# Gates and values of a hybrid decoder block computed first, partly by seven products, and kept in DRAM

## The chip, the core and the metric

The kernel runs on one core of one Trainium2 chip. The core has a matrix engine (TensorE, PE in the profile; its weight loads are listed as PEld), a vector engine (VectorE, DVE), an engine for activation functions (ScalarE, ACT), a general one (GpSimd, POOL) and an engine that mostly issues DMAs (SyncE, SP). Each runs its own instructions in their order; semaphores tie them together. Operands of matmuls lie in SBUF, results in PSUM (eight banks of 128 x 512 floats). Weights stream in from DRAM. The metric is the time of one execution in microseconds on the device; the kernel before takes 1744.1 us, the median of three runs (1743.35 to 1745.33).

## What is computed

One layer for 256 tokens of width 2048, in float32, cut to what matters:

```python
a = rmsnorm(h, norm_mix_pre)
proj = a @ w_in                                   # 2048 x 17408
q_a, k_a, v_a, q_r, f_r, i_r, g_r, gate_a, gate_r = split_columns(proj)
qh, kh, vh = rotary(heads(q_a)), rotary(heads(k_a)), heads(v_a)   # 3 groups x 8 heads x 128
for g, (window, dilation) in enumerate(((128, 1), (512, 4), (2048, 16))):
    o_g, lse_g = dilated_window_attention(qh[g], kh[g], vh[g], window, dilation)
attn = sum over g of softmax(lse over g) * o_g
q = silu(q_r); f = lb + (1 - lb) * sigmoid(f_r)
r = hgrn2_chunked(q, log(f), 1 - f, i_r)          # S_t = diag(f_t) S_{t-1} + k_t v_t, o_t = S_t q_t
r = rmsnorm per head(r) * gain * silu(g_r)
y = sigmoid(gate_a) * (attn @ w_attn_branch) + sigmoid(gate_r) * (r @ w_hgrn_branch)
h = h + rmsnorm(y @ w_mix_out, norm_mix_post)
a = rmsnorm(h, norm_ffn_pre)
h = h + rmsnorm((silu(a @ w_gate) * (a @ w_up)) @ w_down, norm_ffn_post)   # width 5632
```

## The kernel before

**Products in three parts.** Every weight tile is split into a high part (ScalarE, a copy to the matmul type) and a low part (VectorE, the difference), the activations too, and a product is three matmuls: high x high, high x low, low x high. The weights arrive in 512 KB loads from SP into three buffers of 1 MB, are split two steps ahead (`AHEAD`), and are multiplied from three buffers `w`.

**Blocks.** A block is a stretch of columns that owns PSUM banks. Kind "N" (`add`) makes 512 columns with tokens on the partitions: eight steps of 12 matmuls of 128x512. Kind "W" (`add_wide`, two blocks of 256 columns each) makes columns on the partitions and tokens along the row, for f, q of the recurrence and for queries and keys: four steps of 16 matmuls, half of them 512 and half 256 wide; `both_halves` adds the two halves of a bank and hands the result to an evacuation. Blocks of 1024 columns (`add_wide_block`, class `Wide`) are used for up/gate and down. In three of the eight steps of an up/gate block (`GATE_UP`), the two halves of the tokens, the two row tiles and the two column groups form a 2 x 2 product that is made with seven products instead of eight (Strassen's way, Winograd's form): `split_wide` then splits sums of weights as well, `seven_sums` the sums of activations, and `gather` adds the four banks that hold shared products. Such a step has 21 matmuls instead of 24. The down blocks have more of them.

**The order of work.** `chunks` lists the steps of the first half in order, `steps` those of the `Wide` blocks. After each step's matmuls the loop advances the evacuations (`evacs`) and two `lanes` by one `yield` each. A lane holds generators in a row: `opening` (norm of x, tables), the two recurrences (`recurrence(half)`, four heads each), and `attention(half, h)`. Each generator puts a few small instructions on several engines and yields, so that its matmuls fall between the steps of the blocks. The order in the first half is: g (two N blocks), f and q of the recurrence (eight W), inputs i (two N), then for each half of the heads the values of three groups (three N) and queries and keys (twelve W), then the gates (eight N), the branch products, the mix product. The recurrences start when q is done, so the first runs beside i and the values of the first half, the second beside queries and keys of the first half; the attention of a half starts when its last keys are there, the second one beside the gates, whose sigmoids wait until the heads are done (`gate_sigmoids`).

**A level of the recurrence** (`level`, six per recurrence, then `same`, `level64`, `level128`): POOL subtracts (`L769`), ScalarE takes exponentials, VectorE and POOL multiply (`L775`, `L776`), eight small matmuls, VectorE copies under a mask (`L786`). A new level starts every second step.

**Even and odd tokens.** The attention works on even and odd tokens apart. The value blocks therefore read `xT` with a stride of two (`parity=True`), the last addition of the rotation (`evac_rope`, `L683`) writes its result sorted, and the end of a head sorts back. In the rest the token halves are the first and the last 128.

Of the kernel before, what the change touches and what calls it, by code (L numbers as in the profile page):

```python
# [19 lines left out]
P = 128  # L20
# [20 lines left out]
N_RAW, N_SPLIT, AHEAD, WARM, BRIDGE = 6, 3, 2, 8, 6  # L41


class Block:
# [7 lines left out]
    def __init__(self, kind, w, nk, col, xs, evac, parity=False, pre=None, mid=None, post=None):  # L52
        self.kind, self.w, self.nk, self.col = kind, w, nk, col
        self.xs, self.evac, self.parity = xs, evac, parity
        self.pre, self.mid, self.post = pre, mid, post
        self.per = 4 if kind == "W" else 2
        self.width = 1024 // self.per
        self.steps = nk // self.per
        self.banks = None


class Wide:
# [7 lines left out]
    def __init__(self, w, cols, order, xs, seven, evac, prep=None, pre=None, turn=1):  # L70
        self.w, self.cols, self.order, self.xs, self.seven = w, cols, order, xs, seven
        self.evac, self.prep, self.pre, self.turn = evac, prep, pre, turn
        self.last7 = max(i for i, (m, s) in enumerate(order) if s)
        self.bank, self.open, self.rest = {}, set(), None
# [3 lines left out]
def tile_hybrid_block(ctx: ExitStack, tc: tile.TileContext, t, out):  # L78
# [8 lines left out]
    auxp = ctx.enter_context(tc.tile_pool(name="auxp", bufs=4, space=PSUM))  # L87
    ctx.enter_context(tc.manual_schedule())
# [19 lines left out]
    def p3(s, dtype, n, bufs, tag=None):  # L108
        return act_pool[0].tile([P, n], dtype, tag=tag or s, bufs=bufs, name=nm(s))
# [40 lines left out]
    colg = cpool.tile([P, 48], F32, name="colg")  # L150
    r1c = cpool.tile([P, 2], F32, name="r1c")
    r1p = cpool.tile([P, 2], F32, name="r1p")
# [5 lines left out]
    ph1 = ExitStack()  # L158
    kp = ph1.enter_context(tc.tile_pool(name="kp", bufs=1, reuse_waits="tile"))
    fp = ph1.enter_context(tc.tile_pool(name="fp", bufs=1, reuse_waits="tile"))  # L160

    act_pool = []

    def fslot(s):
        return fp.tile([P, 1024], F32, tag="f", bufs=15, name=nm(s))

    def ptile(s):
        pool, n = (act_pool[0], 2) if act_pool else (fp, 5)
        return pool.tile([P, 512], F32, tag="p", bufs=n, name=nm(s))
# [9 lines left out]
    lb = kp.tile([P, 8], F32, name="lb")  # L179
    lb1 = kp.tile([P, 8], F32, name="lb1")  # L180


    blocks, chunks, pairs = [], [], []
    wides, steps = [], []

    def add(*args, **kw):
        b = Block(*args, **kw)
        blocks.append(b)
        for c in range(b.steps):
            chunks.append([b, c, None, None, None])  # L190
# [15 lines left out]
    def parts(j):  # L206

        return (slice(0, 512), slice(512, 1024)) if j == 0 else (slice(0, 1024),)

    def load(j):  # L210
        if j >= len(chunks):
            load_wide(j - len(chunks))
            return
        b, c = chunks[j][:2]
        if j % 2 == 0:
            pairs.append(stream.tile([P, 2048], F32, tag="raw", bufs=N_RAW // 2, name=nm("raw")))
        raw = pairs[j // 2][:, j % 2 * 1024 : j % 2 * 1024 + 1024]
        rows = b.per * P
        src = b.w[c * rows : (c + 1) * rows, b.col : b.col + b.width]
        src = src.rearrange("(k p) c -> p k c", p=P)  # L220
        dst = raw.rearrange("p (k c) -> p k c", k=b.per)
        n = len(parts(j))
        for i in range(n):
            ks = slice(i * b.per // n, (i + 1) * b.per // n)
            nc.sync.dma_start(dst[:, ks, :], src[:, ks, :])
        chunks[j][2] = raw
# [4 lines left out]
    def split(j, only=None):  # L231
        if j >= len(chunks):
            split_wide(j - len(chunks))
            return
        raw = chunks[j][2]
        if chunks[j][3] is None:
            w = wslot()
            chunks[j][3:] = [w[:, :1024], w[:, 1024:]]
        wh, wl = chunks[j][3:]
        for n, k in enumerate(parts(j)):  # L240
# [4 lines left out]
    def multiply(j, sides=(0, 1)):  # L245
        b, c = chunks[j][:2]
        wh, wl = (w.rearrange("p (k c) -> p k c", k=b.per) for w in chunks[j][3:])
        if b.banks is None:
            b.banks = [acc_bank() for _ in range(2)]
        for s in sides:  # L250
            if s == 1 and c == 0 and b.mid:
                b.mid()
            for kk in range(b.per):
# [20 lines left out]
    def add_wide_block(*args, **kw):  # L274
        b = Wide(*args, **kw)
        wides.append(b)
        for i in range(len(b.order)):
            steps.append([b, i, None, None])

    def load_wide(n):  # L280
        if n % 2 or n // 2 >= len(steps):
            return
        n //= 2
        b, i = steps[n][:2]
        m = b.order[i][0]
        raw = stream.tile([P, 2048], F32, tag="raw", bufs=N_RAW // 2, name=nm("raw"))
        for g, col in enumerate(b.cols):
            src = b.w[2 * m * P : (2 * m + 2) * P, col : col + 512]
            nc.sync.dma_start(
                raw[:, g * 1024 : (g + 1) * 1024].rearrange("p (k c) -> p k c", k=2),  # L290
                src.rearrange("(k p) c -> p k c", p=P),
            )
        steps[n][2] = raw

# [1144 lines left out]
```

## Time and profile before

The profiled execution took 1742.44 us, 1740.6 of them inside the span. Stretches of the span, from the windows of the trace:

| us from the start | work | TensorE busy | VectorE busy | ScalarE busy | POOL busy |
|---|---|---|---|---|---|
| 0 to 57 | start, g | 55.4 | 35.8 | 35.7 | 2.8 |
| 57 to 147 | f, q of the recurrence | 90.0 | 55.2 | 43.7 | 0 |
| 147 to 277 | i, first values; first recurrence | 129.7 | 81.9 | 66.0 | 32.9 |
| 277 to 434 | first queries, keys; second recurrence | 155.3 | 127.5 | 71.4 | 34.6 |
| 434 to 521 | second values; attention | 87.0 | 42.9 | 40.1 | 0 |
| 521 to 661 | second queries, keys | 140.0 | 102.4 | 61.3 | 0 |
| 661 to 850 | gates; attention | 189.0 | 93.9 | 87.7 | 0 |
| 850 to 1077 | branches, mix, start of the second half | 224.7 | 143.1 | 112.3 | 3.8 |
| 1077 to 1500 | up and gate, seven products | 423.0 | 368.2 | 228.9 | 0 |
| 1500 to 1741 | down | 231.5 | 214.0 | 139.2 | 0 |

In rows of groups the columns are line, engine, operation, output and inputs, shape, count, busy time and mean in ns, and the idle time before them with what ended it. In rows of the timeline they are start, duration and instruction. A row of the windows gives, after the stretch, its length and the busy time of PE, PEld, VectorE, ScalarE and POOL with their counts, then the granted clock of TensorE, the busy share of the DMA engines and GB/s. In the chain of waits the columns are start, duration and what ran. Float32 matmuls, unlike those of the matmul type, are listed twice.

### The profile page before, as it was taken

To read this page: it belongs to the slowest core of one execution; us is meant where nothing else is said; L and a number is where in the kernel's file an instruction comes from. 1 tells how busy PE (TensorE), PEld (TensorE's weight loads), DVE (VectorE), ACT (ScalarE), POOL (GpSimd) and SP (SyncE) were. 2 spreads that over 40 slices of the span, in tenths; PEclk is the share of its full clock that TensorE was granted. 3 is DMA by queue.
4 is the path that set the end of the run, shared out by engine and by line. 5 is a ranking of instruction groups with operands and counts; after the bars stand their busy time and mean duration, and the time that the engine had idled before them with its cause. 6 is when DMAs were issued, how large, how long until landed. Compare 5 with 4: busy or idle time off the path is not lost.

```text
span 1740.6 us, 21588 instructions
## 1 busy us (share of the span) xinstructions
PE 1725.5 (99%) x8424; PEld 1448.5 (83%) x8424; DVE 1264.6 (73%) x1372; ACT 886.2 (51%) x1050; POOL 74.1 (4%) x54
## 2 busy tenths in 40 slices
PE   9999999999999999999999999999999999999997
PEld 7888888888888888888888877888888888888886
DVE  5657747877546775544566577888888888898998
ACT  6545455344444444454444466555555555665663
POOL 0001413400000000000000000000000000000000
PEclk9999999999999999999999999999999999999999
DMA  7655445445454554445555745655555555666553
GB/s 268 202 194 194 145 149 165 146 157 183 169 167 155 188 193 169 170 169 193 191 180 187 266 166 176 214 198 200 206 194 194 194 194 199 220 209 218 194 198 116
DMA packets 201222, 325.91 MB, mean 187 GB/s; under 512 B 10096, under 2 KB 76832, under 8 KB 201120
## 3 DMA queue, kind: packets, MB, share of 16 engines
q1 hardware_dynamic: 198848, 319.41, 54.3%
q10 hardware_dynamic: 2272, 5.12, 0.8%
q8 instruction: 66, 1.08, 0.3%
q14 instruction: 36, 0.29, 0.1%
HBM read 322.40 MB, written 2.10 MB: 186 GB/s over the span
## 4 chain that ended last, share of the span: by engine, by line
PE 95%; DVE 2%; ACT 1%; DMA 1%; issue 1%; POOL 0%; SPq 0%; DVEq 0%; ACTq 0%
PE acc L115 71%; PE aux L115 22%; DVE w L243 1%; ACT w L242 0%; DVE w L676 0%; PE aux L723 0%; PE aux L452 0%; DMA gpost<-in_norm_mix_post 0%; DMA x<-in_x 0%; PE acc L1126 0%; DVE fz L1255 0%; PE aux L1126 0%; DVE x L775 0%; PE aux L439 0%; ACT junk L1209 0%
## 5 line engine op out<-in xcount | busy, mean ns | idle before, releaser
L243 DVE TENSOR_TENSOR w<-raw,w 128x1024 fp32r<-128x1024 f32 (+1 forms) x353 | 444.6, 1260 | 365.5 <-ACT w L242 363.4
L242 ACT ACTIVATE w<-raw 128x1024 fp32r<-128x1024 f32 (+1 forms) x353 | 373.0, 1057 | 481.6 <-PE acc L115 471.0
L115 PE MATMUL acc<-w,xT 128*128 128x512 f32 x1728 | 407.7, 394 | 0.0
L115 PEld LDWEIGHTS acc<-w,xT 128*128 128x128 f32 x1728 | 325.0, 190 | 65.5
L115 PE MATMUL acc<-xT,w 128*128 128x512 f32 (+1 forms) x2048 | 364.5, 339 | 0.0
L115 PEld LDWEIGHTS acc<-xT,w 128*128 128x128 f32 x2048 | 313.8, 189 | 46.2
L307 DVE TENSOR_TENSOR wl<-raw,w 128x2048 fp32r<-128x2048 f32 x82 | 187.5, 2287 | 34.0 <-ACT w L305 34.0
L305 ACT ACTIVATE w<-raw 128x2048 fp32r<-128x2048 f32 x82 | 156.6, 1910 | 81.7 <-PE aux L115 32.2
L115 PE MATMUL acc<-w,hT 128*128 128x512 f32 x622 | 182.5, 392 | 1.5 <-DVE w L243 1.2
L115 PEld LDWEIGHTS acc<-w,hT 128*128 128x128 f32 x622 | 115.8, 188 | 27.0 <-DVE w L243 2.4
L115 PE MATMUL aux<-w,hT 128*128 128x512 f32 x430 | 135.6, 389 | 0.0
L323 DVE TENSOR_TENSOR wl<-sum,w 128x2048 fp32r<-128x2048 f32 x42 | 96.2, 2290 | 33.8 <-ACT w L319 33.8
L316 ACT ACTIVATE w<-sum 128x1024 fp32r<-128x1024 f32 x42 | 44.7, 1063 | 111.0 <-DVE sum L311 106.7
L115 PEld LDWEIGHTS aux<-w,hT 128*128 128x128 f32 x430 | 80.7, 188 | 16.7
L115 PE MATMUL acc<-w,yT 128*128 128x512 f32 x384 | 88.0, 390 | 0.1
L115 PEld LDWEIGHTS acc<-w,yT 128*128 128x128 f32 x384 | 71.9, 188 | 15.3 <-DVE w L243 0.5
L115 PE MATMUL aux<-w,a 128*128 128x512 f32 x268 | 83.7, 389 | 0.0
L115 PE MATMUL acc<-w,a 128*128 128x512 f32 x268 | 83.6, 389 | 0.0
L115 PE MATMUL aux<-wl,hT 128*128 128x512 f32 x215 | 83.6, 389 | 0.0
L115 PE MATMUL acc<-wl,hT 128*128 128x512 f32 x215 | 83.6, 389 | 0.0
L325 DVE TENSOR_TENSOR dl<-raw,dh 128x1536 fp32r<-128x1536 f32 x42 | 73.6, 1751 | 0.0
L322 ACT ACTIVATE dh<-raw 128x1536 fp32r<-128x1536 f32 x42 | 61.9, 1474 | 0.0
(263 smaller groups left out, 2014.9 us busy)
## 6 DMA issues: line engine op xcount, KB each, us to landing
raw<-in_w_in SPq DMA_DIRECT2D x271, 512.0 KB, 4.5
raw<-in_w_ffn_gate_up SPq DMA_DIRECT2D x176, 512.0 KB, 4.4
raw<-in_w_ffn_down SPq DMA_DIRECT2D x88, 512.0 KB, 4.8
raw<-in_w_mix_out SPq DMA_DIRECT2D x32, 512.0 KB, 4.9
raw<-in_w_attn_branch SPq DMA_DIRECT2D x16, 512.0 KB, 4.7
raw<-in_w_hgrn_branch SPq DMA_DIRECT2D x16, 512.0 KB, 4.5
hx<-in_x ACTq DMA_DIRECT2D x4, 512.0 KB, 9.8
x<-in_x SPq DMA_DIRECT2D x3, 512.0 KB, 10.3
```

The source lines that it names most:

```text
L115: nc.tensor.matmul(ps, lhsT, rhs, start=start, stop=stop, skip_group_check=True)
L242: nc.scalar.activation(wh[:, k], raw[:, k], AF.Copy)
L243: nc.vector.tensor_sub(wl[:, k], raw[:, k], wh[:, k].bitcast(F32))
L305: nc.scalar.activation(hi, raw, AF.Copy)
L307: nc.vector.tensor_sub(lo, raw, hi.bitcast(F32))
L316: nc.scalar.activation(hi[:, :1024], s[:, :1024], AF.Copy)
L322: nc.scalar.activation(dhi, d, AF.Copy)
L323: nc.vector.tensor_sub(lo, s, hi.bitcast(F32))
L325: nc.vector.tensor_sub(dlo, d, dhi.bitcast(F32))
```

## The change

1. Right after g, eight blocks of 1024 columns come first: the four pieces of the two branch gates, the values of the three groups, the inputs i. The first is made of plain steps (`FIRST`), the other seven have the order of the up/gate blocks (`EIGHT`) with three steps of seven products. The sums of activations for three pairs of `xT` are made in a lane by `pair_sums`.
2. Their results, and g, are scaled or passed through the sigmoid (`evac_kept`, ScalarE) and stored to DRAM tiles by ScalarE's queue. They are loaded back by POOL's queue when they are needed (`back`, `values_back`, `gate_back`).
3. Partition p of a token tile now holds the tokens 2p and 2p + 1, so the two token halves are the even and the odd tokens, everywhere. `parity`, `r1p` and the sorting in the rotation and in the attention go; f and q of the recurrence are sorted into time order by their first multiplication, and the recurrence's result back by `put(..., timed=True)`.
4. Queries and keys are made for pairs of heads: per pair three groups of one W block of queries and one of keys, and the attention of a pair starts when its three groups are done. Heads wait in `work` and go to whichever lane is empty; the branch product of the attention asks for them (`heads`).
5. f and q come per half, and each recurrence starts when its own q is done. In a level, one `yield` more stands between the multiplications and the matmuls, and the rotation's two sine products are parted by a `yield`.
6. The branch of the recurrence comes ahead of that of the attention. One list `seq` of `Step`s replaces `chunks` and `steps`. The pools of the first half are opened for two stages, "early" and "middle" (`enter`).

The matrix products are otherwise the same. The core of the diff:

```diff
-H7 = (0, 1, 2)
-GATE_UP = [(3, 0), (4, 0), (0, 1), (5, 0), (1, 1), (6, 0), (2, 1), (7, 0)]
+X7 = H7 = (0, 1, 2)
+FIRST = [(m, 0) for m in range(8)]
+EIGHT = [(3, 0), (4, 0), (0, 1), (5, 0), (1, 1), (6, 0), (2, 1), (7, 0)]
...
                 if b.kind == "N":
                     ps = b.banks[s]
-                    if b.parity:
-                        sh, sl = (
-                            x.rearrange("p (j two) -> p two j", two=2)[:, s, :]
-                            for x in (xh, xl)
-                        )
-                    else:
-                        sh, sl = (x[:, s * P : (s + 1) * P] for x in (xh, xl))
+                    sh, sl = (x[:, s * P : (s + 1) * P] for x in (xh, xl))
...
-    xv = t["x"][0].rearrange("(b p) c -> p b c", p=P)
+    xv = t["x"][0].rearrange("(p b) c -> p b c", b=2)
+    ov = out[0].rearrange("(p b) c -> p b c", b=2)
...
+    def keep(key, width):
+        kept[key] = dram.tile([S, width], F32, name=nm("kept"))
+        return kept[key].rearrange("(p b) c -> p b c", b=2)
+
+    def back(dst, key, lo, hi, timed=False):
+        x = kept[key]
+        x = x.rearrange("(b p) c -> p b c", b=2) if timed else x.rearrange("(p b) c -> p b c", b=2)
+        nc.gpsimd.dma_start(dst, x[:, :, lo:hi])
+
+    def evac_kept(key, fn):
+        def go(b):
+            dst = keep(key, 1024)
+            for s, g in ((0, 0), (0, 1), (1, 0), (1, 1)):
+                src = b.bank[s, g]
+                if b.rest:
+                    e = b.rest[s, g]
+                    nc.vector.tensor_add(e, src, e)
+                    src = e
+                else:
+                    e = eslot()
+                nc.scalar.activation(e, src, fn, scale=r1c[:, s : s + 1])
+                nc.scalar.dma_start(dst[:, s, g * 512 : (g + 1) * 512], e)
+            yield
+        return go
+
+    def end_early():
+        flush(evacs)
+        enter("middle")
+        attnT.append(Split("attnT", 8))
+        recT.append(Split("recT", 8))
+        for half in range(2):
+            gN[half] = hslot("g")
+            back(gN[half], ("g", half), 0, 512, True)
+            iN[half] = hslot("v")
+            back(iN[half], "i", 512 * half, 512 * half + 512, True)
+
+    def values_back(half):
+        for g in range(3):
+            vN[half, g] = hslot("v") if half == 0 and g < 2 else nslot("v")
+            back(vN[half, g], ("v", g), 512 * half, 512 * half + 512)
...
             w = ptile("w").rearrange("p (h t) -> p h t", h=2)
-            for o, n in ((0, 64), (64, 0)):
+            for m, n in ((0, 64), (64, 0)):
                 nc.vector.tensor_mul(
-                    w[o : o + 64], src[n : n + 64],
+                    w[m : m + 64], src[n : n + 64],
                     sin[n : n + 64, None, :].to_broadcast([64, 2, S]),
                 )
+                if m == 0:
+                    yield
...
             nc.vector.tensor_mul(xv[:, :, left], xv[:, :, left], kv[:, :, left])
             nc.gpsimd.tensor_mul(xv[:, :, right], xv[:, :, right], qv[:, :, right])
             yield
+            yield
             ps = aux()
...
+    early = [(COL_GA, ("a", 0), AF.Sigmoid), (COL_GB, ("r", 0), AF.Sigmoid),
+             (COL_GA + 1024, ("a", 1), AF.Sigmoid), (COL_GB + 1024, ("r", 1), AF.Sigmoid)]
+    early += [(COL_V + 1024 * g, ("v", g), AF.Copy) for g in range(3)] + [(COL_IR, "i", AF.Copy)]
+    for n, (col, key, fn) in enumerate(early):
+        add_seven(w_in, (col, col + 512), EIGHT if n else FIRST, xT, lambda m: x7[m],
+                  evac_kept(key, fn), flip=n % 2 == 1, turn=1,
+                  pre=flush_lanes if n == 1 else None)
     for half in range(2):
         add_wide(w_in, KD, COL_FR + 512 * half, xT, evac_f(half))
-    for half in range(2):
-        add_wide(w_in, KD, COL_QR + 512 * half, xT,
-                 evac_qr(half, start_recurrence if half == 1 else None))
-    for half in range(2):
-        add("N", w_in, KD, COL_IR + 512 * half, xT, scaled(iN, half, r1c, hslot))
...
+        if half == 0:
+            blocks[-2].pre = end_early
+        add_wide(w_in, KD, COL_QR + 512 * half, xT, evac_qr(half, start_recurrence(half)))
+    for pair in range(4):
         for g in range(3):
...
+            for o, col, tab in ((0, COL_Q, 0), (2, COL_K, 2)):
+                then = start_attention(pair) if o and g == 2 else None
+                add("W", w_in, KD, col + 1024 * g + 256 * pair, xT,
+                    both_halves(evac_rope((pair, g), o, tab, then), 0))
+    blocks[-3].pre = lambda: (gate_back("r", 0), gate_back("r", 1))
     for j in range(4):
-        add("N", w_in, KD, COL_GA + 512 * j, xT, evac_gate(("a", j), hslot))
+        add("N", t["w_hgrn_branch"][0], 8, 512 * j, lambda k: recT[0](k), evac_rec_branch(j))
+    for j, (key, n) in enumerate((("r", 2), ("a", 0), ("a", 2))):
+        blocks[j - 4].pre = lambda key=key, n=n: (gate_back(key, n), gate_back(key, n + 1))
     for j in range(4):
-        add("N", w_in, KD, COL_GB + 512 * j, xT, evac_gate(("r", j), fslot))
-    for j in range(4):
-        add("N", t["w_attn_branch"][0], 8, 512 * j, attnT, evac_attn_branch(j))
-        add("N", t["w_hgrn_branch"][0], 8, 512 * j, recT, evac_rec_branch(j))
+        add("N", t["w_attn_branch"][0], 8, 512 * j, heads, evac_attn_branch(j))
```

More of the change, by code (lines that the diff above doesn't have):

```diff
@@ L272, in multiply, with split_wide @@
                 mm(b.banks[s][:, :S], l, xh, False, last)
[L274 to L293, printed above, removed]
[L295 to L300 removed]
+    def split_wide(st):
+        b, raw = st.block, st.raw
+        m, by7 = b.order[st.i]
         prep = b.prep(m, by7) if b.prep else iter(())
@@ L496, in advance, with advance_lanes @@
                 return
+    def advance_lanes():
+        for lane in lanes:
+            if not lane and work:
+                lane.append(work.popleft())
+            advance(lane)
     def flush(q):
```

471 lines of the change are left out of this document (229 added, 242 removed).

## The prediction

> **What bounds the kernel now.** I read the page's totals first, then the chain that ended last, then the waits of TensorE, then single stretches.
>
> ```profile
> span 1740.6 us, 21588 instructions
> PE 1725.5 (99%) x8424; PEld 1448.5 (83%) x8424; DVE 1264.6 (73%) x1372; ACT 886.2 (51%) x1050; POOL 74.1 (4%) x54
> ...
> PE 95%; DVE 2%; ACT 1%; DMA 1%; issue 1%; POOL 0%; SPq 0%; DVEq 0%; ACTq 0%
> ```
>
> TensorE is busy 99% of the span and 95% of the chain that ended last is its own work, so a matmul taken away should shorten the run by its own time, and work on another engine is free while it stays under TensorE's time in its stretch. What TensorE still waits for is little; this is the first row of its list of waits (us in total, times, longest):
>
> ```profile
> PE aux L115 <- DVE x L775: 2.1, 3, 1.5
> ```
>
> It belongs to the recurrence (`L775`), and is the place to watch, because the change moves the recurrence.
>
> **What the change takes away.** In program order the main and small matmuls go from 8148 to 8083: 63 of 128x512, and the two 128x1 ones of `opening`. The 63 come from seven blocks of 1024 columns with three such steps each: a step has seven products of three matmuls where eight stood, so 21 steps save three matmuls each. The price of one comes from the up/gate blocks of the second half, which already run in this form:
>
> ```profile
> 1117.87 10.88 PE acc L115 x48
> ...
> 1133.72 7.48 PE acc L115 x33
> ```
>
> 10.88/48 and 7.48/33 are both 0.2267 us. So 63 x 0.2267 = 14.3 us go.
>
> A second gain is in the same matmuls. Six value blocks (576 matmuls) read even or odd tokens of `xT` with a stride of two (`parity=True`); afterwards the token halves lie side by side. Here are a value block and a gate block, each with the same attention pieces between its steps:
>
> ```profile
> 444.28 11.44 PE L115 MATMUL acc<-w,xT 128*128 128x512 f32 x48
> 455.56 1.04 PE L723 MATMUL aux<-ident,p 128*128 128x128 f32 x8
> ...
> 685.85 11.17 PE L115 MATMUL acc<-w,xT 128*128 128x512 f32 x48
> 696.86 1.03 PE L723 MATMUL aux<-ident,p 128*128 128x128 f32 x8
> ...
> 44.75 0.52 PE L115 MATMUL aux<-ident,rowb 128*128 128x1 f32 x4
> 45.13 5.75 PE L115 MATMUL acc<-w,xT 128*128 128x512 f32 x24
> ```
>
> From start to start, 48 strided matmuls take 455.56 - 444.28 = 11.28 us, 48 plain ones 11.01: 5.6 ns each, and 576 of them give 3.2 us. The two tiny matmuls are worth 45.13 - 44.75 = 0.4. Together 17.9 us.
>
> **What it adds to the early blocks.** Each of the seven splits three steps the long way and gathers four banks. The rows of the up/gate blocks price it:
>
> ```profile
> L307 DVE TENSOR_TENSOR wl<-raw,w 128x2048 fp32r<-128x2048 f32 x82 | 187.5, 2287 | 34.0 <-ACT w L305 34.0
> L305 ACT ACTIVATE w<-raw 128x2048 fp32r<-128x2048 f32 x82 | 156.6, 1910 | 81.7 <-PE aux L115 32.2 <-issue 24.5 <-PE acc L115 24.5
> L323 DVE TENSOR_TENSOR wl<-sum,w 128x2048 fp32r<-128x2048 f32 x42 | 96.2, 2290 | 33.8 <-ACT w L319 33.8
> L325 DVE TENSOR_TENSOR dl<-raw,dh 128x1536 fp32r<-128x1536 f32 x42 | 73.6, 1751 | 0.0
> L322 ACT ACTIVATE dh<-raw 128x1536 fp32r<-128x1536 f32 x42 | 61.9, 1474 | 0.0
> L311 DVE TENSOR_TENSOR sum<-raw 128x1024 f32<-128x1024 f32 x42 | 51.1, 1218 | 0.0
> L316 ACT ACTIVATE w<-sum 128x1024 fp32r<-128x1024 f32 x42 | 44.7, 1063 | 111.0 <-DVE sum L311 106.7 <-PE aux L115 4.3
> L318 DVE TENSOR_TENSOR sum<-raw,sum 128x512 f32<-128x512 f32 x42 | 29.1, 692 | 1.4
> L931 ACT ACTIVATE gate<-acc,r1c 128x512 f32<-128x512 f32 x8 | 5.4, 669 | 0.0
> ...
> 1117.87:1160.24 42.37, 42.37 (x193) 35.18 (x192) 36.83 (x31) 22.89 (x20) 0.00 (x0) 1.00 0.58 199
> ```
>
> A block is five plain steps and three long ones. VectorE: 5 x 2.287 + 3 x (1.218 + 2 x 0.692 + 2.290 + 1.751) = 31.4 plus eight adds of the size of `L318` (0.69) in gather and evacuation, 36.9 us. ScalarE: 5 x 1.910 + 3 x (2 x 1.063 + 1.474) = 20.4, plus a copy and four sigmoids or scalings at 0.67, 23.7. TensorE has 183 x 0.2267 = 41.5 us. The last row is one whole up/gate block: VectorE 36.83 of 42.37 us, TensorE busy for all of it. The early blocks put the same load under a block 0.9 us shorter (no transposes of the activations), so I cost them at nothing; the cover is the 4.6 us that VectorE has left in each, and with that gone every further microsecond would be TensorE's.
>
> Four stores of 256 KB per block are issued by ScalarE, in order behind each evacuation, so a late one would hold up the next weight split. They use some 0.46 us of its queue each, by the one row of such an issue, 1.8 us per block against 41.5 - 23.7 = 17.8 free:
>
> ```profile
> 0.73 0.46 ACTq L148 DMA_DIRECT2D rowg<-in_norm_mix_pre  x1
> ...
> hx<-in_x ACTq DMA_DIRECT2D x4, 512.0 KB, 9.8
> ```
>
> The reads back are 18 loads of 512 KB on POOL's queue, of a kind that the trace of before does not have. The nearest row is `hx`: 9.8 us each. Gates are asked for about three blocks (some 33 us of matmuls) before their use; the attention values of the first half some 180 matmuls, 41 us, before the first product that reads them. So a load may take three times that row's time unseen. A lower bound of nothing, an upper one below among the rivals; I take nothing, as `hx` is near. The sums for three pairs of `xT` lie beside the opening blocks, whose plain steps leave VectorE free time, and three more table loads of ScalarE in the middle lie in its idle half (24.72 of 53 us busy in the next row); nothing for either.
>
> **What moves: the recurrences and the attention.** Before, the first recurrence runs beside N blocks (inputs and values), whose evacuation costs VectorE nothing, and the second beside queries and keys, whose rotation costs it much. Afterwards both run beside W blocks, the first beside f, q and the first rotated pair, the second beside rotations and the first attention heads. The second recurrence of before shows what that costs:
>
> ```profile
> 277.00:330.00 53.00, 51.26 (x315) 45.29 (x313) 48.19 (x40) 24.72 (x35) 29.57 (x14) 0.97 0.42 139
> ...
> 297.59 5.80 PE L115 MATMUL acc<-xT,w 128*128 128x512 f32 x32
> 304.85 1.97 PE L115 MATMUL aux<-x 128*128 128x64 f32 x16 [1.47 <-DVE x L775]
> 306.63 7.38 PE L115 MATMUL acc<-xT,w 128*128 128x512 f32 x32
> 313.85 1.90 PE L115 MATMUL aux<-x 128*128 128x64 f32 x16
> 315.56 5.80 PE L115 MATMUL acc<-xT,w 128*128 128x512 f32 x32
> 321.62 1.97 PE L115 MATMUL aux<-x 128*128 128x64 f32 x16 [0.27 <-DVE x L775]
> 323.40 5.89 PE L115 MATMUL acc<-xT,w 128*128 128x512 f32 x32
> 329.13 1.89 PE L115 MATMUL aux<-x 128*128 128x64 f32 x16
> ...
> 295.61 4.14 DVE L676 TENSOR_TENSOR w<-sum,tabs 64x512 f32<-64x512 f32 x2
> ...
> L676 DVE TENSOR_TENSOR w<-sum,tabs x48: 684/686/2405, 295.6 to 658.4; 64x512 f32<-64x512 f32 x48
> ...
> L769 POOL TENSOR_TENSOR x<-b 128x1024 f32<-128x1024 f32 x12 | 30.2, 2518 | 212.9 <-DVE b L761 212.9
> L776 POOL TENSOR_TENSOR x<-x,q 128x512 f32<-128x512 f32 x12 | 17.0, 1416 | 36.6 <-ACT x L773 36.6
> ...
> L710 DVE CUSTOM_DVE_ANT_0 p<-aux,amask 128x512 f32<-128x512 f32 x16 | 10.4, 685 | 0.0
> ```
>
> Two steps of a W block take 329.13 - 323.40 = 5.73 us when nothing is late; the three stretches before take 7.26, 7.22 and 6.06, so 1.5 + 1.5 + 0.3 = 3.3 us were lost, at a granted clock of 0.97. VectorE is 91% busy there. Its rotation products take 4.14 us for two while POOL works, against a median of 0.686 each: POOL's `L769` and `L776` (2.5 and 1.4 us per level) stand in VectorE's way.
>
> The changed order adds a `yield` behind `L775`, so a level's matmuls come one step (2.8 us) later, and parts the two rotation products by a step. That removes the direct wait of 1.47; it does not remove work from VectorE. Beside the second recurrence attention heads now run too. Half a head takes seven steps and costs VectorE `L710`'s 0.69 us and about as much again in its smaller operations, so 0.8 us per W block; over the four to five W blocks of the levels that is 3.6 us on an engine that is 91% busy. Between none and all of it lost, I put the second recurrence at 5 instead of 3.3 us. For the first, whose W blocks of f and q have no rotation until its last third, I take 1 us against 0.35 shown by the row below. Net: 5 + 1 - 3.3 - 0.35 = 2.3 us. Bounds: all stalls vanish (-3.7), or each POOL operation delays VectorE for its whole length (next part).
>
> ```profile
> 172.03 1.97 PE L115 MATMUL aux<-x 128*128 128x64 f32 x16 [0.35 <-DVE x L775]
> ...
> 512.00:675.00 163.00, 163.00 (x933) 142.31 (x932) 113.18 (x146) 72.17 (x96) 0.00 (x0) 1.00 0.55 181
> ```
>
> The second row, W blocks with rotation and attention but no recurrence, has TensorE busy throughout with VectorE at 69%; the later pairs should run so. The last two heads fall into the branch blocks of the recurrence, with at least 12 matmuls, 2.7 us, between their steps; I add 0.3 for the last copy.
>
> **Sum.** The profiled execution took 1742.4 us (span 1740.6 and 1.8 around it). 1742.4 - 17.9 + 2.3 + 0.3 = 1727.1. The median of the runs shown is 1.7 us above it, so on the median's scale I predict 1728.5.
>
> **Rivals.**
> 1. *VectorE behind POOL through both recurrences* (slower). If VectorE has no slack beside a level, the level costs TensorE the whole of POOL's 2.518 + 1.416 = 3.93 us; twelve levels are 47.2 us, 43.5 above the 3.7 already paid: 1742.4 - 17.9 + 43.5 = 1768, 1770 on the median's scale. It decides from (17.9 + 3.7) / 3.93, so between five and six of the twelve levels paid in full. For it: 4.14 us for two rotation products, and rotations now beside one recurrence and a third of the other. Against it: before, the three fully loaded stretches of two steps lost 3.3 us together, less than one level in full, since splits run two steps ahead. A quarter of it, 12 us, gives 1742.4 - 17.9 + 8 = 1733, 1734 on the median's scale.
> 2. *The loads on POOL's queue come late* (slower or same). Three value loads in a row at 9.8 us are 29 of the 41 us available; at five times the row's time TensorE would stand still some 100 us at the first product with values: 1825. At one and a half times it loses 3: 1731. Against it: the DMA share of 0.42 and 0.55 in the rows of the middle above.
> [...]
> 3. *The early blocks do not hold the pace* of the up/gate blocks, because ScalarE waits behind its own stores: 18 free us per block against 1.8 speak against it. A microsecond lost at each of the 21 long steps takes back the gain: 1727.1 + 21 = 1748, 1750 on the median's scale; half of that is 1739.
> 4. *The stalls go altogether*, through the added `yield`: 1742.4 - 17.9 - 3.7 = 1720.8, 1722.5 on the median's scale.
>
> **How the numbers follow.** Forecast (1724 to 1735): 0.60. Rival 4: 0.16. Rival 1 in full: 0.10, rival 2: 0.05, rival 3: 0.09. What a measurement can tell from no change is 0.2%, 3.5 us. Faster: forecast, rival 4 and a little of rivals 2 and 3, 0.80; same 0.06; slower 0.14. The range reaches from a little under rival 4 over the halves of rivals 1 to 3 and leaves out their full prices: 1719 to 1742.
>
> **What would show it.** Right: seven early blocks each 41.5 us long with no TensorE idle, value blocks at 0.2267 us per matmul, VectorE near 89% there, and TensorE waits only beside POOL's work in the two recurrences, 4 to 8 us in all. Wrong: TensorE idle at `recT`, at values or gates with a DMA as releaser (rival 2); ScalarE idle before a weight split in the early blocks (rival 3); VectorE's rotation products at 2 us in most of the W blocks beside both recurrences and TensorE waiting for splits (rival 1).

## The result and the profile after

The changed kernel is slower: 1753.9 us (median of six runs, 1753.3 to 1755.2) against 1743.8 for the kernel before (six runs, 1742.2 to 1746.4). The ratio is 1.0058 with a 95% interval of 1.0048 to 1.0069. The prediction was 1728.5, with a range that ended at 1742.

The page's totals and its chain that ended last, for the changed kernel:

```profile
span 1751.3 us, 21627 instructions
PE 1716.4 (98%) x8357; PEld 1438.6 (82%) x8357; DVE 1382.7 (79%) x1457; ACT 925.6 (53%) x1051; POOL 92.5 (5%) x72
...
PE 90%; DVE 4%; ACT 2%; issue 1%; POOL 1%; DMA 0%; ACTq 0%; SPq 0%; DVEq 0%; POOLq 0%
```

TensorE has less work, as it should (1716 against 1725 us busy), but its share of the chain fell from 95% to 90%. Its waits (us in total, times, longest), where one row of 2.1 us led before:

```profile
PE aux L133 <- DVE qk L784: 7.4, 3, 6.7
PE acc L133 <- DVE w L298: 4.2, 6, 1.3
PE aux L133 <- POOL x L949: 3.7, 1, 3.7
PE aux L482 <- DVE y L1039: 3.6, 4, 0.9
PE acc L133 <- ACT w L297: 2.3, 2, 1.8
PE aux L133 <- DVE wl L333: 1.8, 1, 1.8
```

All of the difference lies in the first half. These are the timelines of TensorE at the first up/gate matmul, before and after; the distance is 11.2 us, and the spans differ by 10.7:

```profile
1075.31 0.39 PE L115 MATMUL aux<-w,hT 128*128 128x512 f32 x1
```

```profile
1086.48 0.39 PE L133 MATMUL aux<-w,hT 128*128 128x512 f32 x1
```

**The early blocks ran as foretold.** The windows of the changed kernel (length, busy PE, PEld, VectorE, ScalarE, POOL, granted clock, DMA share, GB/s):

```profile
106.97:397.32 290.35, 290.35 (x1282) 240.45 (x1281) 245.39 (x195) 159.78 (x133) 0.00 (x0) 1.00 0.64 225
```

For seven blocks of 183 matmuls, 290.4/1281 = 0.2267 us each, TensorE never stood still, with VectorE at 85%. The page's list of DMA issues has the loads back (KB each, median us to landing):

```profile
v<-kept POOLq DMA_DIRECT2D x8, 512.0 KB, 6.3
gate<-kept POOLq DMA_DIRECT2D x8, 512.0 KB, 6.2
```

No wait of TensorE names a load of `kept`, in the rows above or in the rest of the list. So the loss lies around the early blocks, at four places.

**Place 1, the opening.**

```profile
46.97:61.21 14.24, 11.92 (x37) 8.71 (x37) 9.96 (x25) 7.88 (x11) 0.85 (x1) 0.76 0.47 161
46.97:50.29 3.32, 1.00 (x2) 0.38 (x2) 1.53 (x3) 2.64 (x4) 0.00 (x0) 0.82 0.21 79
50.29:55.00 4.71, 4.71 (x11) 3.75 (x12) 4.64 (x10) 0.21 (x1) 0.00 (x0) 0.50 0.68 223
```

In 14.24 us TensorE does 11.92 us of work, 4.7 of them at a granted clock of 0.50. ScalarE's timeline there, with the idle time and its cause in brackets:

```profile
47.25 0.36 ACTq L756 DMA_DIRECT2D kept<-g  x1
47.65 0.38 ACT L524 ACTIVATE rowb<-aux 128x256 f32<-128x256 f32 x1 [5.30 <-DVE g L755]
...
55.67 0.63 ACT L413 ACTIVATE so<-s 128x512 fp32r<-128x512 f32 x1 [5.17 <-DVE s L412]
```

ScalarE stands 5.3 us behind its own store of g, whose data VectorE has not made, and later 5.2 us behind the copy of the sums. The weight splits behind them in its queue are late. VectorE in turn begins that part of g at 46.52 us, after 2.25 us of idleness, at about the time at which the gain row came (its load was issued at 40.76 and took 5.7 us). The first block behind g starts at 61.21 us here and at 56.57 us in the kernel before, and TensorE stands another 1.8 us in it for the split of `L333`.

**Place 2, the first recurrence.** The window, then rows of the timelines of ScalarE, VectorE and TensorE, all of the changed kernel:

```profile
470.81:523.00 52.19, 45.31 (x274) 39.59 (x273) 38.60 (x35) 27.12 (x36) 24.57 (x11) 0.93 0.38 122
```

```profile
471.82 0.63 ACT L718 ACTIVATE f<-f 128x512 f32<-128x512 f32 x1 [3.56 <-DVE f L717]
...
505.79 0.63 ACT L735 ACTIVATE sig<-q 128x512 f32<-128x512 f32 x1 [4.50 <-DVE q L734]
```

```profile
475.95 1.76 DVE L298 TENSOR_TENSOR w<-raw,w 128x1024 fp32r<-128x1024 f32 x1 [4.17 <-ACT w L297]
```

```profile
477.76 2.85 PE L133 MATMUL acc<-xT,w 128*128 128x256 f32 x15 [1.30 <-DVE w L298]
...
513.63 3.57 PE L133 MATMUL aux<-ones,x 128*128 128x1 f32 x16 [3.73 <-POOL x L949]
```

One chain: ScalarE waits 3.6 us for VectorE's product, then VectorE waits 4.2 us for ScalarE's next split, then TensorE 1.3 for VectorE's. The last row belongs to the sigmoid at 505.79: POOL's product of `L949` stands behind one that needs exponentials, which ScalarE makes after that sigmoid, and TensorE waits 3.7 us for it. ScalarE is busy for 27 of the 52 us and VectorE for 39; neither is full, and what stands behind what in their queues sets the pace.

**Place 3, the first attention head.** TensorE waits 6.7 us for the rotated queries and keys. Timelines of TensorE, VectorE and POOL:

```profile
603.69 0.79 PE L133 MATMUL aux<-qk 128*128 128x128 f32 x2 [6.70 <-DVE qk L784]
604.14 5.19 PE L133 MATMUL acc<-xT,w 128*128 128x512 f32 x16
```

```profile
595.30 2.28 DVE L776 TENSOR_TENSOR w<-sum,tabs 64x512 f32<-64x512 f32 x1
...
599.36 1.98 DVE L783 TENSOR_TENSOR sum<-sum,tabs 128x512 f32<-128x512 f32 x1
601.37 2.26 DVE L784 TENSOR_TENSOR qk<-sum,w 128x512 f32<-128x512 f32 x1
```

```profile
594.16 2.88 POOL L865 TENSOR_TENSOR x<-b 128x1024 f32<-128x1024 f32 x1
598.45 2.34 POOL L872 TENSOR_TENSOR x<-x,q 128x512 f32<-128x512 f32 x1 [1.41 <-ACT x L869]
600.75 2.34 POOL L865 TENSOR_TENSOR x<-b 128x1024 f32<-128x1024 f32 x1
```

The three steps of the rotation take 2.0 to 2.3 us each while POOL works, instead of 0.69 (as in the run with POOL's work on VectorE below), and the last of them has 0.93 in the mean of all its executions:

```profile
L784 DVE TENSOR_TENSOR qk<-sum,w 128x512 f32<-128x512 f32 x24 | 22.2, 925 | 0.9
```

**Place 4, the turn of y.** The row of `L1039` above: four waits of 0.9. The changed kernel hands y to its transposes (`turns.append`) in the step in which VectorE still adds it, where the kernel before did so one step later. That line is not among those of the change shown ahead of the prediction.

### The profile page after: what moved, and what is told of

The parts are those of the page before. It is cut to its first block, busy times and chain, and to the rows that moved or that the text cites. A ratio compares the mean times of both kernels' runs of the same rounds, so it can differ in the third digit from the quotient of the medians.

```text
span 1751.3 us, 21627 instructions
## 1 busy us (share of the span) xinstructions
PE 1716.4 (98%) x8357; PEld 1438.6 (82%) x8357; DVE 1382.7 (79%) x1457; ACT 925.6 (53%) x1051; POOL 92.5 (5%) x72
## 4 chain that ended last, share of the span: by engine, by line
PE 90%; DVE 4%; ACT 2%; issue 1%; POOL 1%; DMA 0%; ACTq 0%; SPq 0%; DVEq 0%; POOLq 0%
PE acc L133 57%; PE aux L133 32%; DVE w L298 1%; ACT w L297 1%; PE aux L821 0%; PE aux L494 0%; DVE x L871 0%; POOL x L865 0%; PE acc L1178 0%; DVE fz L1305 0%; DVE b L857 0%; DMA x<-in_x 0%; PE aux L1178 0%; PE aux L482 0%; DVE sum L783 0%
## 5 line engine op out<-in xcount | busy, mean ns | idle before, releaser
L298 DVE TENSOR_TENSOR w<-raw,w 128x1024 fp32r<-128x1024 f32 (+1 forms) x225 | 279.3, 1243 | 194.2 <-ACT w L297 193.7
L297 ACT ACTIVATE w<-raw 128x1024 fp32r<-128x1024 f32 (+1 forms) x225 | 236.1, 1053 | 254.0 <-PE acc L133 228.0
L333 DVE TENSOR_TENSOR wl<-raw,w 128x2048 fp32r<-128x2048 f32 x125 | 285.7, 2287 | 62.1 <-ACT w L331 61.1
L331 ACT ACTIVATE w<-raw 128x2048 fp32r<-128x2048 f32 x125 | 238.7, 1910 | 129.8 <-PE aux L133 60.0
L349 DVE TENSOR_TENSOR wl<-sum,w 128x2048 fp32r<-128x2048 f32 x63 | 144.4, 2291 | 65.0 <-ACT w L345 64.9
L133 PE MATMUL acc<-w,xT 128*128 128x512 f32 x536 | 158.2, 398 | 2.3 <-ACT w L297 1.8
L133 PEld LDWEIGHTS acc<-w,xT 128*128 128x128 f32 x536 | 101.9, 192 | 24.5 <-ACT w L297 2.0
L133 PE MATMUL aux<-w,xT 128*128 128x512 f32 x386 | 121.1, 390 | 0.0
L351 DVE TENSOR_TENSOR dl<-raw,dh 128x1536 fp32r<-128x1536 f32 x63 | 110.3, 1751 | 0.0
L133 PEld LDWEIGHTS aux<-w,xT 128*128 128x128 f32 x386 | 72.4, 188 | 15.3 <-ACT w L331 0.3
```

The costliest lines, as they stand in the source:

```text
L133: nc.tensor.matmul(ps, lhsT, rhs, start=start, stop=stop, skip_group_check=True)
L297: nc.scalar.activation(wh[:, k], raw[:, k], AF.Copy)
L298: nc.vector.tensor_sub(wl[:, k], raw[:, k], wh[:, k].bitcast(F32))
L331: nc.scalar.activation(hi, raw, AF.Copy)
L333: nc.vector.tensor_sub(lo, raw, hi.bitcast(F32))
L349: nc.vector.tensor_sub(lo, s, hi.bitcast(F32))
```

## The experiments

Eleven kernels ran in three groups, each beside the kernel before, whose medians were 1743.1, 1742.9 and 1743.5. Differences are to that median.

| run | edit | us | to before | ratio, 95% interval |
|---|---|---|---|---|
| the change | | 1753.9 | +10.1 | 1.0048 to 1.0069 |
| g store | store on POOL's queue | 1751.6 | +8.6 | 1.0032 to 1.0065 |
| sigmoid | later by a step | 1741.2 | -1.9 | 0.9981 to 0.9999 |
| head | first one three steps later | 1753.1 | +10.0 | 1.0041 to 1.0071 |
| turn | later by a step | 1750.3 | +7.2 | 1.0026 to 1.0056 |
| opening | three edits | 1746.6 | +3.7 | 1.0011 to 1.0030 |
| plain | no seven products early | 1764.1 | +21.2 | 1.0107 to 1.0138 |
| sigmoid, levels | and POOL's work on VectorE | 1735.6 | -7.3 | 0.9944 to 0.9974 |
| three | sigmoid, turn, opening | 1728.6 | -14.3 | 0.9902 to 0.9935 |
| three, levels | and POOL's work on VectorE | 1723.6 | -19.9 | 0.9874 to 0.9901 |
| all parts | and the head later | 1726.3 | -17.1 | 0.9887 to 0.9915 |
| before, levels | before, POOL's work on VectorE | 1743.2 | -0.3 | 0.9989 to 1.0007 |

**The store of g alone.**

```diff
-                nc.scalar.dma_start(there[:, i, :], dst[:, i, :])
+                nc.gpsimd.dma_start(there[:, i, :], dst[:, i, :])
```

> g is stored by POOL's queue instead of ScalarE's. Theory: in the opening, ScalarE stands behind its own store of g, which waits for VectorE's g, which waits for the gain row; the weight splits behind it come late. Then TensorE's stops near 47, 49 and 61 us go, its clock stays at 1.00 there, the first early block starts some 6 to 7 us sooner, and the time falls from 1753.9 to about 1747. Rival: the opening is short of VectorE and ScalarE time (sums of activations, table loads); then the stops move a little and the time falls by 2 us at most.

It gave 1.5 us, which the two intervals do not tell from nothing. ScalarE no longer waits for the store, but it stands at the next thing that is late; its timeline in this run:

```profile
54.29 0.63 ACT L413 ACTIVATE so<-s 128x512 fp32r<-128x512 f32 x1 [8.23 <-DVE s L412]
```

**The sigmoid one step later.** In the evacuations of f and q (the lines of q are shown; f has the same added line):

```diff
             nc.vector.tensor_mul(in_time(d), by_side(src), by_side(by_rows(rowb, 2)))
+            yield
             nc.scalar.activation(s, d, AF.Sigmoid)
```

> One yield between the multiplication by the row norm and the sigmoid, in the evacuations of f and q. Theory: beside the first recurrence ScalarE stands 4 to 5 us at each of these sigmoids, because VectorE's product is still behind other work, and POOL, the exponentials and the splits wait behind it; with the yield these waits go, and of the 9.8 us lost between 470 and 523 us no more than 2 stay: about 1746. [...]

12.0 us, the largest single part. The same stretch in the windows of this run, and ScalarE's timeline at the first of the sigmoids:

```profile
470.81:523.00 52.19, 52.09 (x338) 46.71 (x337) 46.38 (x46) 31.45 (x41) 29.05 (x15) 1.00 0.45 146
```

```profile
472.35 0.63 ACT L719 ACTIVATE f<-f 128x512 f32<-128x512 f32 x1 [0.74 <-DVE f L717]
472.99 1.28 ACT L870 ACT_TABLE_LOAD   x1
```

TensorE is busy throughout, VectorE does 46 us of work in the stretch in which it had done 39, and the clock is full. The wait of 3.56 is 0.74. The table loads are still there, like the one in the last row, so it was not they that cost.

**The first head later.**

```diff
         while (head // 4, 2) not in vN:
             yield
+        if head == 0:
+            yield
+            yield
+            yield
```

> The first head of attention starts three yields later. Theory: its first products stand 6.7 us at the rotated keys that VectorE finishes late, and TensorE's clock falls for some us after that; three steps (8.5 us of matmuls) cover it: 8 to 9 us less, about 1745. Rival: VectorE stays as late as it is (POOL beside it), so TensorE waits at the next small product or split instead: 0 to 3 us less.

Nothing gained. The waits of this run:

```profile
PE acc L133 <- DVE w L298: 7.1, 9, 1.3
...
PE aux L133 <- DVE x L875: 1.8, 2, 1.5
```

The wait for q and k is down to 0.7 us, but the splits now come late instead (4.2 before the edit). VectorE was behind, and whatever TensorE asked of it first had to wait. The theory that the head was merely started a step too early fell.

**The turn one step later.**

```diff
-                if i == 1:
-                    turns.append(yT[0].turned(y, 2 * j, 2))
                 yield
+            turns.append(yT[0].turned(y, 2 * j, 2))
```

> The transposes of y start one step later, as in the kernel before. Theory: each of the four waits of 0.9 us (1.2 us from start to start) for the last addition goes: 4 to 5 us less, about 1749. Rival: a later transpose makes yT late for the mix product, which takes the gain back: no change.

2.9 us, and the four waits are gone. The intervals of the two kernels overlap a little, and the traces give a larger size: from the first matmul of the branches to the first one of up/gate it is 1084.02 - 843.54 = 240.5 us here and 1086.48 - 841.38 = 245.1 us in the changed kernel, 4.6 us less. This execution lost 2.9 us ahead of f, where the two kernels are the same: f starts at 400.25 us instead of 397.32.

**The opening.** The load of the gain row stands behind half of the squares of x in the program, and on POOL's queue; the store of g as above; and a step between VectorE's sums and ScalarE's copy of them (`sums_made` is `seven_sums` without that copy):

```diff
-            seven_sums(f, dst)()
+            s = sums_made(f)
+            yield
+            nc.scalar.activation(dst[:, 0], s, AF.Copy)
+            nc.vector.tensor_sub(dst[:, 1], s, dst[:, 0].bitcast(F32))
...
-        yield from sumsq(ss, xt)
-        nc.sync.dma_start(gainr, t["hgrn_norm_gain"].to_broadcast([P, HW]))
+        yield from sumsq(ss, xt[:2])
+        nc.gpsimd.dma_start(gainr, t["hgrn_norm_gain"].to_broadcast([P, HW]))
+        yield from sumsq(ss, xt[2:], 2)
```

> Three edits in the opening: the gain row is loaded by POOL's queue after half of the squares instead of by SP behind the weights, g is stored by POOL's queue, and a yield stands between VectorE's sums for a pair of xT and ScalarE's copy of them. Theory: with g's store away from ScalarE, the copies of the sums (8 us of waiting in one row) and the late gain row (2 us on VectorE) are what keeps the splits late; with all three gone the stops before the first early block shrink from 5 us (and the lower clock after them) to 1 or 2, and the time is 1746 to 1748. Rival: the first splits of 2048 columns are themselves too long for a stretch of 2.7 us steps: the 1.8 us wait for VectorE's low part and the loss of 3 us around it stay, 1750 to 1752.

6.4 us. Its windows:

```profile
46.97:61.21 14.24, 14.24 (x63) 11.19 (x62) 13.27 (x26) 9.45 (x10) 0.54 (x1) 1.00 0.69 220
```

63 matmuls lie in the stretch that held 37, and f starts at 391.90 us instead of 397.32, 5.4 us earlier. The edit does two things more. On POOL's queue nothing holds the load of the gain row back, so it is issued at once, beside the loads of x and of the first weights; rows of POOL and TensorE in this run:

```profile
2.53 0.69 POOL L597 DMA_DIRECT2D gainr<-in_hgrn_norm_gain  x1
9.97 0.63 PE L502 MATMUL aux<-ident,x 128*128 128x128 f32 x4 [3.15 <-DMA x<-in_x]
```

In the profiles of the four kernels with this edit that wait for x is 2.8 to 3.2 us, in the changed kernel and those without the edit 0.2 to 1.6. And `pair_sums` makes the sums of `h` in the second half as well. The windows from a matmul that both runs have there to the first one of up/gate, in the changed kernel and in this one:

```profile
1036.33:1086.48 50.15, 48.66 (x223) 38.80 (x224) 39.56 (x67) 35.64 (x61) 3.69 (x5) 1.00 0.47 160
1030.45:1078.47 48.02, 47.72 (x224) 39.09 (x224) 39.08 (x67) 35.79 (x61) 3.71 (x5) 1.00 0.52 170
```

So 2.1 us of this edit's gain have nothing to do with the opening. The kernel before has the same two waits for a split there (0.4 and 0.8 us), and could have had this gain too. Which of the edits made the rest was not parted, beyond the store alone.

**Without the seven products.** All early blocks in the plain form:

```diff
-X7 = H7 = (0, 1, 2)
+X7, H7 = (), (0, 1, 2)
...
-        add_seven(w_in, (col, col + 512), EIGHT if n else FIRST, xT, lambda m: x7[m],
+        add_seven(w_in, (col, col + 512), FIRST, xT, lambda m: x7[m],
```

> All eight early blocks are made of plain steps, and no sums of xT are made; everything else as in the changed kernel. The 63 matmuls come back: +14.3 us where TensorE sets the pace of these blocks. Theory: 1753.9 + 14.3 - 1 to 4 (the sums no longer disturb the opening) = 1764 to 1767. Rival, that the seven-product blocks do not reach TensorE's pace and their saving is lost: 1754 to 1758.

11.1 us slower than the change. The 63 matmuls are worth 14.3 by the row. The windows from the first matmul of the early blocks to the first one of f, in this run and in the changed kernel:

```profile
58.29:408.71 350.42, 348.60 (x1538) 288.40 (x1537) 151.79 (x70) 146.00 (x99) 0.00 (x0) 1.00 0.68 222
61.21:397.32 336.11, 334.28 (x1474) 276.59 (x1474) 271.91 (x209) 181.49 (x148) 0.00 (x0) 1.00 0.66 230
```

350.42 - 336.11 = 14.3 us, as priced. The missing 3.2 us lie in the opening, where the sums are no longer made: the plain kernel reaches the early blocks 2.9 us sooner. (The profiles of the kernels with the opening of the change reach them at 61.2 to 64.2 us.)

**POOL's two operations of a level on VectorE**, on top of the sigmoid:

```diff
-            nc.gpsimd.tensor_sub(xv, bv, bv[:, :, w - 1 : w].to_broadcast([P, n, 2 * w]))
+            nc.vector.tensor_sub(xv, bv, bv[:, :, w - 1 : w].to_broadcast([P, n, 2 * w]))
...
-            nc.gpsimd.tensor_mul(xv[:, :, right], xv[:, :, right], qv[:, :, right])
+            nc.vector.tensor_mul(xv[:, :, right], xv[:, :, right], qv[:, :, right])
```

> With the yield before the sigmoids, the subtraction and the right-hand multiplication of the six levels of each recurrence run on VectorE instead of POOL. If POOL holding VectorE off is what makes VectorE late beside the recurrences, its rotation products fall from 2 us to 0.7 there, the wait for rotated keys (5.3 us with the yield alone) goes below 1, and the time is 1733 to 1736 against 1741.2 with the yield alone. If VectorE is simply full there, the added 2 us of its own per level make it later: 1741 to 1750.

5.4 us faster than the sigmoid alone (-7.3 against -1.9 in the table), although VectorE, the engine that was late, has 24 operations more. VectorE's timeline in this run, before the first head:

```profile
582.25 1.23 DVE L867 TENSOR_TENSOR x<-b 128x1024 f32<-128x1024 f32 x1
...
587.60 0.69 DVE L786 TENSOR_TENSOR qk<-sum,w 128x512 f32<-128x512 f32 x1
```

The last step of the rotation is back at 0.69 us, and TensorE's wait for it is 1.3 us (5.3 with the sigmoid alone). The two operations take 1.2 and 0.7 us on VectorE and 2.8 and 1.7 on POOL, in the mean. This settles place 3: POOL's operations hold VectorE up for longer than the work itself takes there, by 1.3 to 1.6 us in each of the three steps (2.0 to 2.3 against 0.69).

**The three edits together.** The diffs of the sigmoid, the turn and the opening, in one kernel.

> The yield before the sigmoids, the later transposes of y and the three edits of the opening together. If their gains are separate they add: 1753.9 - 12 (sigmoids) - 3.6 (y) - 6 (opening) = 1732. If one lost time covers another, 1736 to 1740.

24.4 us less than the change, more than the 21.3 of the three singly; by the traces the turn alone is 4.6 instead of 2.9, which is over half of the difference. What is left is TensorE's wait for the first head; rows of TensorE and VectorE:

```profile
587.55 0.80 PE L133 MATMUL aux<-qk 128*128 128x128 f32 x2 [5.28 <-DVE qk L795]
```

```profile
585.63 1.86 DVE L795 TENSOR_TENSOR qk<-sum,w 128x512 f32<-128x512 f32 x1
```

**The three and the levels on VectorE.** The diff of POOL's two operations on top of that.

> The three edits together (the yield before each sigmoid, the opening's gain row and sums, the heads' turn after the last yield), and the two POOL operations of a level on VectorE as well. If VectorE's lateness beside the second recurrence comes from POOL, the 5.3 us wait of TensorE for the first head's q and k goes and with it what the clock adds: 5 to 7 us below the 1728.6 of the three edits alone, 1722 to 1724. If VectorE is simply full there (it has 12 operations more now, about 1.2 us each per level at most), the wait stays and the time is 1728 to 1731.

5.6 us below the three, and the fastest of all. The same wait is now

```profile
582.60 0.49 PE L133 MATMUL aux<-qk 128*128 128x128 f32 x2 [1.24 <-DVE qk L795]
```

and VectorE's group of that line, 0.93 us in the mean in the changed kernel, has 0.73:

```profile
L795 DVE TENSOR_TENSOR qk<-sum,w 128x512 f32<-128x512 f32 x24 | 17.6, 732 | 0.9
```

Most of the gain lies at this wait: from the first matmul of f to the one that waits it is 587.55 - 393.96 = 193.6 us in the kernel with the three edits and 582.60 - 393.52 = 189.1 us here. The second recurrence behind it, from its first level's matmuls to those of `ones`, takes 36.3 us there and 36.7 us here.

**And the head later.** The diff of the first head on top of both.

> The kernel with levels on VectorE and the three edits, and the first attention head three steps later. If nothing waits for the first head any more, the three steps are worth nothing: within 1 us of the kernel beside it. If 1 to 2 us of wait for q and k are left there, it is 1 to 2 us faster. If the head's work then falls on steps that are fuller, it is 1 to 3 us slower.

Its runs (1723.5 to 1728.2) overlap those of the kernel without it (1722.7 to 1725.0), and its median is 2.7 us higher: no gain, perhaps a loss. In its profile TensorE waits 0.7 us for q and k instead of 1.9, but 1.5 us for a split that was in time before. The start of the first head is not worth moving.

**The levels on VectorE in the kernel before.** The same two operations there, `L769` and `L776`.

> The kernel before, with the two POOL operations of a level on VectorE. It lost 3.7 us beside both recurrences. If POOL's hold on VectorE is what is lost there, 2 to 4 us go: 1739 to 1741. If the hold hurts only where the attention's first head runs beside the recurrence, which is so after the change alone, it stays within 1.5 us of 1743. If VectorE is too full there to take twelve levels more (about 1.2 us each), it is 2 to 8 us slower.

No difference. TensorE's wait for a level's own product stays (2.4 us in all; 2.1 with POOL), and no first head follows the rotation there. POOL's hold on VectorE cost nothing in this kernel; that it costs only where VectorE's products are waited for at once fits both kernels, but was not tried by itself.

## Why the prediction was wrong

1. *The gain of 17.9 us*: its main term is shown. The step without seven products takes 14.3 us more in the stretch of the early blocks, which is the price of the 63 matmuls, and their window bears out 0.2267 us each, in the blocks of values too. The stride's 3.2 us was not tried by itself. (The last addition is off: 1727.1 + 1.7 is 1728.8, not 1728.5.)
2. *The early blocks at nothing beside the pace of TensorE* held, and rival 3 with its stores of `kept` fell there: no wait in 290 us.
3. *The loads back at nothing* held. They landed in 6.2 and 6.3 us, below the 9.8 taken, and rival 2 fell.
4. *The second recurrence at 5 us* was near in size: VectorE behind POOL. Taking POOL's operations away is worth 5.4 and 5.6 us in the two pairs of runs, most of it at the first head's wait (4.5 of the 5.6). The prediction spread the loss over the levels; the `yield` it counted on did remove the wait for a level's product (0.2 us instead of 2.1). Rival 1 named the mechanism, but for all twelve levels; at its price of 3.93 us per level, 1.4 levels were paid. Of the 3.3 us that the prediction read as lost beside the second recurrence before, the 1.5 of the stretch of 7.22, in which TensorE waits for nothing, were not VectorE's lateness: 3.2 us of that stretch ran at a granted clock of 0.50, behind the wait of 1.47 (last section).
5. *"The sums for three pairs of `xT` lie beside the opening blocks, whose plain steps leave VectorE free time"*: this step failed. The three edits take 5.4 us out of the time up to f in the profile, although they add 2.9 us of waiting for x; of their 6.4 us in the table, 2.1 belong to the sums of `h`. VectorE's free time was counted, but not that ScalarE, which must split the weights, stands in order behind the store of g and the copy until VectorE has made what they read. The prediction did say that a late store would hold up the next split, and looked for it in the early blocks only (rival 3).
6. *"For the first, whose W blocks of f and q have no rotation until its last third, I take 1 us"*: this step failed, by 12.0 us, the greatest miss. It was looked at as a load on VectorE. The price was in ScalarE's order: a sigmoid that is issued in the same step as VectorE's product stands in front of the next split. The three table loads at nothing were right; with the sigmoid moved they remain and TensorE does not wait. Before, f and q ran without a recurrence beside them, so that VectorE made the product soon: ScalarE stood 2.1 us at each of these sigmoids instead of 3.6 to 4.6, and TensorE did not wait.
7. *The turn of y* was not in the sum at all: 2.9 us by the medians, 4.6 by the traces, from a line that moved by one step.

Points 5 to 7 together are 21.3 us singly and 24.4 in one kernel. Without the 2.1 us at the sums of `h`, which are no cost of the change, 22.3 of the 25.7 us between forecast and result are accounted for (15.6 below and 10.1 above the kernel before). Most of the rest, 2.7 us, is the longer wait for x that the edits themselves bring. The opposite side of the forecast was given a chance of 0.14, all of it to mechanisms that did not decide where they were placed. The one that did, an engine half idle in its totals and blocked in its queue, was in rival 3 for the early blocks, and for none of the places where it happened. Rival 4, without any stall, gave 1722.5, and the kernel with the three edits and the levels moved takes 1723.6, with the 2.1 us at the sums of `h` to its credit.

## What to carry to other kernels

A share of busy time says little of an engine that works in order for two customers (ScalarE, busy for 27 of the 52 us of place 2, where a later sigmoid gave 12.0): for each instruction that is moved beside other work, ask what stands behind it in its queue while it waits for another engine, and put a step between two engines' parts of one evacuation. When a wait goes away and the time does not (the waits for q and k fell from 7.4 us to 0.7, and the time only from 1753.9 to 1753.1), look for an engine that is behind altogether; the next request pays. Work that a slower engine seems to take off a busy one can cost the busy one more than doing it itself (POOL's two operations of a level, 5.4 and 5.6 us here), and only a run without it tells. And an edit of a helper acts wherever the helper is called: look at every stretch of the span before its gain is put down to one.

## What was not expected of the hardware

A wait of TensorE can cost more than its length, in one place here by 2.2 us. After the 6.70 us for q and k, the windows of the changed kernel show the next stretch at a granted clock of 0.50, and the same after the opening's waits (shown above, 0.50 from 50.29 to 55.00), but not after the one wait of 1.8 us for the split of `L333`, which ends at 63.54. The last row is of the kernel before, behind the wait of 1.47 us at 304.85 that the prediction shows:

```profile
63.54:70.00 6.46, 6.46 (x28) 5.36 (x29) 4.44 (x2) 4.80 (x4) 0.00 (x0) 1.00 0.86 303
604.14:607.00 2.86, 2.86 (x11) 2.47 (x11) 2.51 (x6) 0.32 (x1) 0.00 (x0) 0.50 0.00 0
...
307.30:310.50 3.20, 3.20 (x11) 2.71 (x10) 3.20 (x6) 0.00 (x0) 0.00 (x0) 0.50 0.53 168
```

TensorE's timeline at a place without a wait, and the end of the 16 matmuls that follow the wait of 6.70 us:

```profile
499.44 5.90 PE L133 MATMUL acc<-xT,w 128*128 128x512 f32 x32
505.18 1.89 PE L133 MATMUL aux<-x 128*128 128x64 f32 x16
...
609.16 1.90 PE L133 MATMUL aux<-x 128*128 128x64 f32 x16
```

Undisturbed, 32 matmuls take 505.18 - 499.44 = 5.74 us, so 16 take 2.87; after the wait 16 take 609.16 - 604.14 = 5.02, which is 2.2 us more. The length of a wait does not tell these places apart: in the opening the lower clock begins inside the stretch of 3.32 us from 46.97 to 50.29 (its mean is 0.82), which held 1.00 us of work between waits of 1.9 and 0.5 us; in the kernel before, 0.50 came behind a single wait of 1.47 us; and behind the wait of 1.8 us that ends at 63.54 the clock is 1.00. What sets it no run here shows.

Three operations of VectorE took about three times as long beside POOL's. In the rows of place 3, 0.69 us became 2.0 to 2.3 beside POOL's 2.3 to 2.9; each of the three starts after the operation of POOL that it overlaps and ends about 0.55 us behind it (597.58 and 597.04, 601.34 and 600.79, 603.63 and 603.09). By what means POOL holds VectorE up there no run here shows.
